# A two-layer hybrid model on one core: tiles in multiples of 64 bytes, a rewritten first phase, retention products in split form, and lower weight parts set 32 bytes further on

## The chip, the core and the metric

The program runs on one core of a Trainium2 chip. The metric is the device time of one execution in microseconds. The profile shows the engines TensorE (PE; its weight loads are listed apart as PEld), VectorE (DVE), ScalarE (ACT), GpSimd (POOL) and SyncE (SP, which here only issues transfers), and the DMA engines.

## What is computed

Two transformer layers on 256 tokens with 2048 features, batch 1, all in float32. Cut to what matters:

```python
def reference(x, mem, positions, ...):
    mem_n = _rmsnorm(mem, norm_mem)
    h = x
    for l in range(2):
        hn = _rmsnorm(h, norm_mix[l])
        if l == 0: h = h + _mixer_ab(hn, ...)  # 8 block-attention heads and 8 sparse-attention heads, then w_out_ab
        else:      h = h + _mixer_c(hn, ...)   # 8 retention heads: q, k of 256, v of 512 features, then w_out_c
        h = h + _cross_attn(_rmsnorm(h, norm_cross[l]), mem_n, ...)  # 4 heads on 256 memory rows
        h = h + _conv_ffn(_rmsnorm(h, norm_ffn[l]), ...)             # 2048 -> 2 x 5632, width-3 convolution, gate, -> 2048
    return _rmsnorm(h, norm_final)
...
    def step(state, xs):                       # retention, chunks of 128 tokens
        qi, ki, vi = xs
        intra = einsum('bhnm,bhmv->bhnv', einsum('bhnd,bhmd->bhnm', qi, ki) * decay, vi)
```

## The kernel before

Every weight is streamed from HBM once. A float32 product is made of three matmuls in the type float32r. `weights` loads a tile of 128 x 1024 values (`raw`), ScalarE rounds it to its upper part (`hi`, L232) and VectorE takes the rest as its lower part (`lo`, L233). Activations are split likewise into one slab of 128 x 512 values per 128 features: 256 columns (tokens) of the upper part, 256 of the lower. The names of tiles in a profile are all "t"; "acc" is a pair of accumulators in PSUM for the big products, "bank" a PSUM tile for the small ones.

There are two forms of a product. In `product_b` the weights are stationary: the upper part is loaded as weights and the whole slab of 512 columns streams past it (L272, upper times upper and upper times lower); then the lower part is loaded, and only the 256 columns of the slab's upper part stream past (L277). Eight slabs make a chunk: 16 matmuls of L272 and 16 of L277, in turns. In `product_a` the slab is stationary, and the weights' upper, lower and upper part stream past it (L307, L308, L309), with 512 columns, or with 256 and 280 in the first two products of the first layer. Small products (transposes, attention, retention) use plain float32, of which each matmul shows as two records in the trace (the transposes as one).

The tile allocator places tiles at multiples of 32 bytes. As built, slabs and weight parts all begin 32 bytes past a multiple of 64. In the product of 280 columns, weights lie 1120 bytes apart in a tile, so that they start in turns at 32 and at 0 past a multiple of 64.

**First phase** (L363 to L414). Two products with w_in_ab (columns 4096 to 4607, the compressed keys' and values' inputs) run in step with the loading of x. `SPANS` gives pairs of slabs; for each pair x and the weights are loaded on SP's queue, x is split (L197 on ScalarE, L200 on VectorE), the weights are split (L401, L406, L407), and `first` issues the pair's matmuls. From the ninth slab on, x is loaded ahead, and weights come four slabs at a time. The results leave the accumulators by `halves` (L326 on ScalarE, L328 on VectorE). The two products use all four accumulators, so the product behind them (columns 4864, L307) waits for `halves`. The order of ScalarE, VectorE and TensorE is that of the code here, and in the rest of the program TensorE's is, while the other engines' order is the scheduler's.

**Side work.** `side` is a queue of generators; `run` advances the first n of them by one step after each step of the big product, and so their small matmuls stand between the big ones. `start_steps` loads the rows of x for the first norm (`load_rows`), sums their squares (`norm.add`, L148), and builds tables; `compress`, `nsa_group`, `nsa_head` and `angle_steps` are such generators.

**Retention** (`mixer_c`). Per head `ev_v` brings v out of PSUM (L963) and subtracts its mean (L965). `attend` makes the scores (L975, L977), multiplies them by the decay (L979, L980), and multiplies scores and v in float32 (L986, L988).

Of the kernel before, what the change touches and what calls it, by code (L numbers as in the profile page):

```python
# [20 lines left out]
P = 128  # L21
# [54 lines left out]
def hybrid_kernel(ctx: ExitStack, tc: tile.TileContext, a, out):  # L76
# [33 lines left out]

    ident = new([P, P])
    make_identity(nc, ident)
    ones = new([P, P])
    pool.memset(ones, 1.0)
# [98 lines left out]


# [150 lines left out]
    SPANS = [range(k, k + 2) for k in range(0, ND, 2)]  # L365
# [5 lines left out]
    def load_x(p):  # L371

        nc.sync.dma_start(x_in[p].rearrange("p s t -> p (s t)"), a["x"][:, 2 * p * S : (2 * p + 2) * S])
# [5 lines left out]
    with tc.manual_schedule(engines=engines):  # L379
        act.activation(new([P, 1]), eps, AF.Copy, scale=eps)  # L380
        load_par(nc.sync, "mix")
        for p in range(ND // 2):
            i, c = p // 2, slice(p % 2 * 512, p % 2 * 512 + 512)
            if p % 2 == 0:
                raws = [raw_tile() for _ in range(2)]
                his = [new([P, 1024], F32R, "whi", 4) for _ in range(2)]
                los = [new([P, 1024], F32R, "wlo", 4) for _ in range(2)]
            if p < 4:
                load_x(p)
            for q in range(2):  # L390
                if p < 4 or p % 2 == 0:
                    d = c if p < 4 else slice(0, 1024)
                    nc.sync.dma_start(raws[q][:, d], w_ab.part(4 * i, 4, 4096 + 256 * q, 256)[:, d])
            if p == 3:
                for x in range(4, 8):
                    load_x(x)
            for s in (2 * p, 2 * p + 1):
                xs_mix.append(slab_tile())
                xhat_hi(xs_mix[s], x_in[p][:, s % 2, :], gain("mix")[:, s : s + 1])
            if p == 0:  # L400
                dve.tensor_copy(his[0][:, c], raws[0][:, c])  # L401
            for s in (2 * p, 2 * p + 1):
                xhat_lo(xs_mix[s], x_in[p][:, s % 2, :], gain("mix")[:, s : s + 1])
            for q in range(2):
                if p or q:
                    act.activation(his[q][:, c], raws[q][:, c], AF.Copy)  # L406
                dve.tensor_sub(los[q][:, c], raws[q][:, c], his[q][:, c].bitcast(F32))  # L407
# [3 lines left out]
            if p == 3:  # L411
# [126 lines left out]
    def cross(l, xs, norm, head_done):  # L538
# [24 lines left out]
        for blk in range(2):  # L563
            run(product_b_steps(weights(w_q, 0, ND, 2 * P * blk, 2 * P), xs, ev_q), n=4)
# [52 lines left out]
    def mixer_ab(xs, row, col, kcv):  # L617
# [6 lines left out]
        def start_steps():  # L624
            norm = Norm()
            tg = [(t, g) for g in range(4) for t in range(2)]
            for i in range(10):
                if i < 8:
                    load_rows(*tg[i])
                if i > 1:  # L630
                    norm.add(*tg[i - 2])
                if i < 9:
                    yield
# [8 lines left out]
            yield from angle_steps(0, posi)  # L642
# [19 lines left out]
        def compress(i, kind, t, done):  # L662

            for _ in range(8):
# [79 lines left out]
        side.extend((start_steps(), setup_steps()))  # L744
# [23 lines left out]
        def nsa_group(g, qr, qu):  # L768
# [34 lines left out]
            yield  # L803
            yield
            yield
# [4 lines left out]
            dve.tensor_copy(pct, b[:, 0:S])  # L810
            pcts[g] = pct

        def nsa_head(g, r, q):
# [9 lines left out]
            while len(comp) < 2:  # L823
# [104 lines left out]
    def mixer_c(xs, norm, done):  # L928
# [25 lines left out]
        def head(h, os):  # L954
# [4 lines left out]
            v = [long(), long()]  # L959

            def ev_v(t, acc):
                sm = small(1)
                act.activation(v[t], acc, AF.Identity, scale=norm.c[:, t : t + 1], accum_out=sm)  # L963
                dve.tensor_scalar_mul(sm, sm, -1.0 / 512)
                dve.tensor_scalar_add(v[t], v[t], sm)  # L965
# [247 lines left out]
```

## Time and profile before

| | before |
|---|---|
| median of 3 runs | 2832.78 us (2832.66 to 2833.45) |
| the profiled execution | 2834.51 us, span 2832.8 us, mean granted clock 0.998 |
| TensorE busy | 2812.4 us of the span, 14726 matmuls |
| VectorE, ScalarE busy | 1906.3 us, 1460.1 us |
| DMA | 530.11 MB, mean 187 GB/s |

Matmuls are pipelined, and their ends are modelled: the time that one costs in a stream is the distance to the start of the next, not its duration. A row of the timeline gives start, duration, engine, line, operation, tiles and shapes, the number of merged instructions and, in brackets, the idle time before and what ended it.

### The profile page before, as it was taken

How to read it: one execution, taken by the hardware profiler on the slowest of the kernel's cores; microseconds unless marked ns; L12 is line 12 of the kernel's file. 1: busy time of each engine (PE TensorE's matmuls, PEld its weight loads, DVE VectorE, ACT ScalarE, POOL GpSimd, SP SyncE). 2: the span in 40 equal slices, each digit the busy share in tenths (PEclk: the TensorE clock that was granted, in tenths of full speed). 3: DMA queues.
4: the chain of work that ended last, by engine and by line, in shares of the span. 5: the costliest groups of instructions: out<-in, count | busy, mean ns of one | idle time of the engine just before them, and what ended most of it. 6: DMA issues, size and time to landing. Idle time of an engine off the chain costs nothing.

```text
span 2832.8 us, 39488 instructions
## 1 busy us (share of the span) xinstructions
PE 2812.4 (99%) x14726; PEld 2406.5 (85%) x14726; DVE 1906.3 (67%) x3147; ACT 1460.1 (52%) x2193; POOL 29.9 (1%) x211
## 2 busy tenths in 40 slices
PE   8999999999999999999999999999999999999998
PEld 7888888888888888888888888888888888888887
DVE  7765776776767677665555555556767767676766
ACT  6454455654545455454444444444665645454544
POOL 0000000000000000000000000000000000000000
PEclk9999999999999999999999999999999999999999
DMA  8535565455555555555555555555545555555554
GB/s 305 171 126 161 180 211 172 170 189 192 187 198 190 189 196 201 194 179 179 179 178 186 193 178 179 182 206 189 189 164 193 186 196 184 193 193 187 197 186 158
DMA packets 150544, 530.11 MB, mean 187 GB/s; under 512 B 17040, under 2 KB 17456, under 8 KB 150352
## 3 DMA queue, kind: packets, MB, share of 16 engines
q1 hardware_dynamic: 148752, 523.65, 54.7%
q0 software_dynamic: 1024, 2.90, 0.3%
q8 instruction: 115, 1.88, 0.3%
q10 hardware_dynamic: 576, 1.05, 0.1%
q14 instruction: 77, 0.63, 0.1%
HBM read 525.43 MB, written 2.10 MB: 186 GB/s over the span
## 4 chain that ended last, share of the span: by engine, by line
PE 98%; DMA 1%; ACT 0%; DVE 0%; SPq 0%; issue 0%; ACTq 0%; DVEq 0%
PE acc L272 32%; PE acc L277 17%; PE acc L307 14%; PE acc L309 14%; PE acc L308 14%; PE bank L350 1%; PE bank L986 0%; DMA t<-in_w_in_ab_dram 0%; PE bank L504 0%; PE bank L496 0%; PE bank L484 0%; DMA t<-in_rows_dram 0%; PE bank L1009 0%; PE bank L589 0%; PE bank L579 0%; PE bank L975 0%
## 5 line engine op out<-in xcount | busy, mean ns | idle before, releaser
L233 DVE TENSOR_TENSOR t<-t,t 128x1024 fp32r<-128x1024 f32 x954 | 1156.6, 1220 | 568.7 <-ACT t L232 522.9
L232 ACT ACTIVATE t<-t 128x1024 fp32r<-128x1024 f32 x954 | 1004.6, 1057 | 739.6 <-PE acc L309 540.6
L272 PE MATMUL acc<-t,t 128*128 128x512 f32 x4096 | 965.9, 391 | 6.2 <-DVE t L200 6.2
L272 PEld LDWEIGHTS acc<-t,t 128*128 128x128 f32 x4096 | 759.7, 188 | 159.1 <-DVE t L200 6.2
L307 PE MATMUL acc<-t,t 128*128 128x512 f32 (+2 forms) x1824 | 713.3, 391 | 4.9 <-DVE t L328 4.9
L309 PE MATMUL acc<-t,t 128*128 128x512 f32 (+2 forms) x1824 | 705.1, 387 | 0.0
L308 PE MATMUL acc<-t,t 128*128 128x512 f32 (+2 forms) x1824 | 704.5, 386 | 0.0
L277 PEld LDWEIGHTS acc<-t,t 128*128 128x128 f32 x4096 | 510.6, 192 | 11.6 <-issue 0.4
L277 PE MATMUL acc<-t,t 128*128 128x256 f32 x4096 | 518.0, 283 | 0.0
L307 PEld LDWEIGHTS acc<-t,t 128*128 128x128 f32 x1824 | 343.9, 189 | 74.7 <-DVE t L328 5.4
L309 PEld LDWEIGHTS acc<-t,t 128*128 128x128 f32 x1824 | 343.6, 188 | 69.5
L308 PEld LDWEIGHTS acc<-t,t 128*128 128x128 f32 x1824 | 343.9, 189 | 68.9 <-issue 1.9
L883 ACT ACTIVATE t<-acc 128x256 f32<-128x256 f32 x176 | 65.8, 374 | 229.6 <-PE acc L272 229.6
L886 DVE TENSOR_TENSOR t<-acc,t 128x256 f32<-128x256 f32 x176 | 74.1, 421 | 157.2 <-ACT t L883 157.2
L889 ACT ACTIVATE t<-t,t 128x256 f32<-128x256 f32 x176 | 103.8, 590 | 1.1
L210 ACT ACTIVATE t<-t 128x256 fp32r<-128x256 f32 x88 | 36.1, 411 | 130.5 <-DVE t L908 130.5
L607 DVE TENSOR_TENSOR t<-t,acc 128x512 f32<-128x512 f32 x148 | 95.1, 680 | 2.8 <-PE acc L1104 2.8
L891 DVE SCALAR_TENSOR_TENSOR t<-t,t,t 128x256 f32<-128x256 f32 x176 | 84.2, 478 | 1.5
L890 DVE SCALAR_TENSOR_TENSOR t<-t,t,t 128x256 f32<-128x256 f32 x176 | 84.2, 478 | 0.2
L326 ACT ACTIVATE t<-acc 128x256 f32<-128x256 f32 x80 | 30.0, 376 | 103.4 <-PE acc L272 103.4
L328 DVE TENSOR_TENSOR t<-acc,t 128x256 f32<-128x256 f32 x80 | 33.4, 419 | 69.7 <-ACT t L326 69.7
L887 DVE TENSOR_TENSOR t<-t,t 128x256 f32<-128x256 f32 x176 | 74.3, 422 | 3.0
(218 smaller groups left out, 1127.6 us busy)
## 6 DMA issues: line engine op xcount, KB each, us to landing
t<-in_w_up_dram SPq DMA_DIRECT2D x352, 512.0 KB, 3.4
t<-in_w_in_c_dram SPq DMA_DIRECT2D x192, 512.0 KB, 3.5
t<-in_w_down_dram SPq DMA_DIRECT2D x176, 512.0 KB, 3.4
t<-in_w_in_ab_dram SPq DMA_DIRECT2D x80, 512.0 KB, 4.2
t<-in_w_out_c_dram SPq DMA_DIRECT2D x64, 512.0 KB, 3.3
t<-in_w_out_ab_dram SPq DMA_DIRECT2D x32, 512.0 KB, 4.2
t<-in_w_kv_x_dram SPq DMA_DIRECT2D x32, 512.0 KB, 3.8
t<-in_w_q_x_dram SPq DMA_DIRECT2D x16, 512.0 KB, 3.2
```

What stands on the lines that cost most here:

```text
L232: act.activation(hi[:, 0 : m * ncol], raw[:, 0 : m * ncol], AF.Copy)
L233: dve.tensor_sub(lo[:, 0 : m * ncol], raw[:, 0 : m * ncol], hi[:, 0 : m * ncol].bitcast(F32))
L272: pe.matmul(acc[j], parts[k - k0][0][:, j * P : (j + 1) * P], xs[k], start=(k == 0), stop=(end and k == n - 1))
L277: pe.matmul(acc[j][:, 0:S], parts[k - k0][1][:, j * P : (j + 1) * P], xs[k][:, 0:S], start=False, stop=(end and k == n - 1))
L307: pe.matmul(o, xh, hi, start=(k == 0), stop=False)
L308: pe.matmul(o, xh, lo, start=False, stop=False)
L309: pe.matmul(o, xl, hi, start=False, stop=(k == n - 1))
L607: dve.tensor_add(part(t, g), part(t, g), acc)
L887: dve.tensor_mul(u[:, 2:], t, norm.r)
L889: act.activation(c, u[:, 2:], AF.Identity, bias=cp[:, 3, j : j + 1], scale=cp[:, 2, j : j + 1])
L890: dve.scalar_tensor_tensor(c, u[:, 1 : S + 1], cp[:, 1, j : j + 1], c, op0=ALU.mult, op1=ALU.add)
L891: dve.scalar_tensor_tensor(c, u[:, 0:S], cp[:, 0, j : j + 1], c, op0=ALU.mult, op1=ALU.add)
```

## The change

Four things change.

1. `new` rounds the rows of two-dimensional tiles up to a multiple of 64 bytes. As built, slabs and weight parts now begin at a multiple of 64 bytes. `part_tile` makes the split weights' tiles, and in `product_b` and in the first phase the lower parts begin 8 values (32 bytes) into theirs; upper parts and all parts in `product_a` do not.
2. The first phase: eight matmuls of ones run ahead; the first two spans are single slabs; x and weights are loaded span by span in the order of use, the first weights on ScalarE's queue.
3. Side work: the rows' loads begin one step later and their sums four steps later; `angle_steps` becomes a generator of its own behind `setup_steps`; `compress` begins six steps earlier; `nsa_group` and `nsa_head` yield at other places.
4. Retention: v and the decayed scores are split into upper and lower parts, and each float32 matmul becomes three in float32r.

```diff
     def new(shape, dt=F32, tag=None, bufs=1):
...
+        unit = 64 // mybir.dt.size(dt)
+        if len(shape) == 2 and shape[1] % unit:
+            full = [shape[0], -(-shape[1] // unit) * unit]
+            return sb.tile(full, dt, name=name, tag=tag or name, bufs=bufs)[:, 0 : shape[1]]
...
+    def part_tile(tag, shift=0):
+        return new([P, 1040 if tag == "wlo" else 1024], F32R, tag, 4)[:, shift : shift + 1024]
...
-    def weights(w, s0, ns, c0, ncol):
+    def weights(w, s0, ns, c0, ncol, shift=0):
...
-            raw, hi, lo = raw_tile(), new([P, 1024], F32R, "whi", 4), new([P, 1024], F32R, "wlo", 4)
+            raw, hi, lo = raw_tile(), part_tile("whi"), part_tile("wlo", shift)
...
     def product_b(w, xs, c0, evac, s0=0, n=2):
-        run(product_b_steps(weights(w, s0, len(xs), c0, 2 * P), xs, evac), n=n)
+        run(product_b_steps(weights(w, s0, len(xs), c0, 2 * P, 8), xs, evac), n=n)
...
-    SPANS = [range(k, k + 2) for k in range(0, ND, 2)]
+    SPANS = [range(0, 1), range(1, 2)] + [range(k, k + 2) for k in range(2, ND, 2)]
...
+        warm = bank()
+        for _ in range(8):
+            pe.matmul(warm[:, 0:P], ones, ones, start=True, stop=True)
...
+        for ks in SPANS:
...
+            load_x(ks[0], ks[0] + m)
             for q in range(2):
...
+                (nc.sync if ks[0] else nc.scalar).dma_start(raws[q][:, d], w_ab.part(ks[0] // 4 * 4, 4, 4096 + 256 * q, 256)[:, c])
+            if ks[0] == 0:
+                load_par(nc.sync, "mix")
...
         def start_steps():
...
-            for i in range(10):
-                if i < 8:
-                    load_rows(*tg[i])
-                if i > 1:
-                    norm.add(*tg[i - 2])
-                if i < 9:
-                    yield
+            for i in range(14):
+                if 0 < i < 9:
+                    load_rows(*tg[i - 1])
+                if i > 5:
+                    norm.add(*tg[i - 6])
+                yield
...
         def compress(i, kind, t, done):
-            for _ in range(8):
+            for _ in range(2):
                 yield
...
-            v = [long(), long()]
+            vh, vl = [[new([P, 512], F32R, *tag) for _ in range(2)] for tag in (("vh", 2), ("long", 9))]
 
             def ev_v(t, acc):
-                sm = small(1)
-                act.activation(v[t], acc, AF.Identity, scale=norm.c[:, t : t + 1], accum_out=sm)
+                sm, v = small(1), new([P, 512], F32, "p", 7)
+                act.activation(v, acc, AF.Identity, scale=norm.c[:, t : t + 1], accum_out=sm)
                 dve.tensor_scalar_mul(sm, sm, -1.0 / 512)
-                dve.tensor_scalar_add(v[t], v[t], sm)
+                act.activation(vh[t], v, AF.Identity, bias=sm)
+                dve.scalar_tensor_tensor(vl[t], v, sm, vh[t].bitcast(F32), op0=ALU.add, op1=ALU.subtract)
...
+                ph, pl = new([P, 512], F32R, "p", 7), new([P, 512], F32R, "p", 7)
+                act.activation(ph[:, 0 : S + P], pr[:, 0 : S + P], AF.Copy)
+                dve.tensor_sub(pl[:, 0 : S + P], pr[:, 0 : S + P], ph[:, 0 : S + P].bitcast(F32))
...
-                    pe.matmul(b, pr[:, t * P : (t + 1) * P], v[0], start=True, stop=(t == 0))
-                    if t:
-                        pe.matmul(b, pr[:, S : S + P], v[1], start=False, stop=True)
+                    blocks = [(t * P, 0), (S, 1)][: t + 1]
+                    for c0, i in blocks:
+                        for p_, v_ in ((ph, vh), (ph, vl), (pl, vh)):
+                            pe.matmul(b, p_[:, c0 : c0 + P], v_[i], start=(i == 0 and p_ is ph and v_ is vh),
+                                      stop=(c0 == blocks[-1][0] and p_ is pl))
```

Where the change moves instructions, the order of an engine's queue shows it. First SP's queue at the very start, before the change (t_72 holds the gains, t_75 and t_76 are x, t_92 and t_93 the raw weights of the two products):

```order
L128 DMA t_72<-in_par_dram 128x32
L373 DMA t_75<-in_x_dram 128x512
L393 DMA t_92<-in_w_in_ab_dram 128x512
L393 DMA t_93<-in_w_in_ab_dram 128x512
L373 DMA t_76<-in_x_dram 128x512
```

and with it (L381 loads x, L133 the gains, L408 the weights):

```order
L381 DMA t_75<-in_x_dram 128x256
L133 DMA t_72<-in_par_dram 128x32
L381 DMA t_75<-in_x_dram 128x256
L408 DMA t_102<-in_w_in_ab_dram 128x256
L408 DMA t_103<-in_w_in_ab_dram 128x256
```

x now stands ahead of the gains, and the first slab's two weight loads have left SP's queue for ScalarE's, where they are the first two instructions.

Next ScalarE's queue at the end of the first phase, before (L148 sums the squares of a row tile, t_73 and t_74 are the rows; L232 splits weights; L326 evacuates an accumulator):

```order
L148 ACTIVATE t_464,t_408<-t_74 128x512 [waits DMAHW6_49]
L148 ACTIVATE t_485,t_408<-t_73 128x512 [waits DMAHW7_49]
L232 ACTIVATE t_391<-t_390 128x1024 [waits DMAHW0_49,DVE_49,PE_49]
L148 ACTIVATE t_500,t_408<-t_74 128x512 [waits DMAHW2_49]
L232 ACTIVATE t_431<-t_430 128x1024 [waits DMAHW1_49,DVE_49,PE_49]
L148 ACTIVATE t_521,t_408<-t_73 128x512 [waits DMAHW4_49]
L148 ACTIVATE t_538,t_408<-t_74 128x512 [waits DMAHW5_49]
L326 ACTIVATE t_346<-acc_111 128x256 [waits PE_49]
L326 ACTIVATE t_350<-acc_112 128x256 [waits PE_49]
```

and with the change (L153, L241 and L335 are these three lines now):

```order
L421 ACTIVATE t_307<-t_348 128x512 [waits DMAHW3_49]
L241 ACTIVATE t_415<-t_414 128x1024 [waits DMAHW4_49,DVE_49,PE_49]
L153 ACTIVATE t_550,t_432<-t_73 128x512 [waits DMAHW5_49]
L335 ACTIVATE t_370<-acc_117 128x256 [waits PE_49]
L241 ACTIVATE t_454<-t_453 128x1024 [waits DMAHW6_49,DVE_49]
L335 ACTIVATE t_374<-acc_118 128x256 [waits PE_49]
L153 ACTIVATE t_573,t_432<-t_74 128x512 [waits DMAHW7_49]
L153 ACTIVATE t_606,t_432<-t_73 128x512 [waits DMAHW0_49]
```

One sum of squares stands ahead of the first evacuation now, where six did (one of them earlier than the rows shown).

Last TensorE's queue at the products of scores and v in one head, before:

```order
L986 MATMUL bank2611_12704<-t2563_12479,t2603_12664 128x512 [waits DVE_49]
L986 MATMUL bank2613_12709<-t2563_12479,t2603_12664 128x512
L988 MATMUL bank2613_12709<-t2564_12480,t2603_12664 128x512 [waits DVE_49]
L307 MATMUL acc2598_12639<-t2622_12735,t2465_12053 128x512 [waits Activation_49]
```

and with it (t2613 and t2614 are the scores' upper and lower part, t2568 and t2570 those of v's first half, t2569 and t2571 of its second):

```order
L1008 MATMUL bank2622_12738<-t2568_12503,t2613_12697 128x512 [waits Activation_49]
L1008 MATMUL bank2622_12738<-t2570_12505,t2613_12697 128x512 [waits DVE_49]
L1008 MATMUL bank2622_12738<-t2568_12503,t2614_12698 128x512 [waits DVE_49]
L1008 MATMUL bank2624_12745<-t2568_12503,t2613_12697 128x512
L1008 MATMUL bank2624_12745<-t2570_12505,t2613_12697 128x512
L1008 MATMUL bank2624_12745<-t2568_12503,t2614_12698 128x512
L1008 MATMUL bank2624_12745<-t2569_12504,t2613_12697 128x512
L1008 MATMUL bank2624_12745<-t2571_12506,t2613_12697 128x512
L1008 MATMUL bank2624_12745<-t2569_12504,t2614_12698 128x512
```

Three matmuls have become nine at the same place, and the first ones now wait for ScalarE's and VectorE's splits.

More of the change, by code (lines that the diff above doesn't have):

```diff
@@ L108, in slab_tile @@
         return new([P, 2 * S], F32R, "xs", 32)
+    ones = new([P, P])
+    pool.memset(ones, 1.0)
     ident = new([P, P])
     make_identity(nc, ident)
-    ones = new([P, P])
-    pool.memset(ones, 1.0)
     eps = new([P, 1])
@@ L379, in hybrid_kernel @@
     with tc.manual_schedule(engines=engines):
[L380 to L384, printed above, removed]
+        warm = bank()
+        for _ in range(8):
+            pe.matmul(warm[:, 0:P], ones, ones, start=True, stop=True)
+        raws = [None, None]
+        for ks in SPANS:
+            p, m = ks[0] // 2, len(ks)
+            c = slice(ks[0] % 4 * 256, ks[0] % 4 * 256 + 256 * m)
+            if ks[0] % 4 == 0:
+                his = [part_tile("whi") for _ in range(2)]
+                los = [part_tile("wlo", 8) for _ in range(2)]
+            if ks[0] in (0, 4, 14):
                 raws = [raw_tile() for _ in range(2)]
[L386 to L389, printed above, removed]
+            elif ks[0] in (8, 10, 12):
+                raws = [new([P, 512], F32, "p", 7) for _ in range(2)]
+            d = slice(0, 512) if ks[0] in (8, 10, 12) else c
+            load_x(ks[0], ks[0] + m)
             for q in range(2):
[L391 to L397, printed above, removed]
+                (nc.sync if ks[0] else nc.scalar).dma_start(raws[q][:, d], w_ab.part(ks[0] // 4 * 4, 4, 4096 + 256 * q, 256)[:, c])
+            if ks[0] == 0:
+                load_par(nc.sync, "mix")
+                act.activation(new([P, 1]), eps, AF.Copy, scale=eps)
+            for s in ks:
                 xs_mix.append(slab_tile())
@@ L400, in hybrid_kernel @@
             if p == 0:
-                dve.tensor_copy(his[0][:, c], raws[0][:, c])
-            for s in (2 * p, 2 * p + 1):
+                dve.tensor_copy(his[0][:, c], raws[0][:, d])
+            for s in ks:
                 xhat_lo(xs_mix[s], x_in[p][:, s % 2, :], gain("mix")[:, s : s + 1])
@@ L563, in cross @@
         for blk in range(2):
-            run(product_b_steps(weights(w_q, 0, ND, 2 * P * blk, 2 * P), xs, ev_q), n=4)
+            run(product_b_steps(weights(w_q, 0, ND, 2 * P * blk, 2 * P, 8), xs, ev_q), n=4)
         while len(xm) < ND:
@@ L641, in start_steps @@
                     dve.tensor_mul(kcv[i][:, j, :], held[i][j], row)
-            yield from angle_steps(0, posi)
             dve.tensor_copy(cos_k, row)
@@ L802, in nsa_group @@
             side.extend(nsa_head(g, r, qr[r]) for r in range(4))
-            yield
-            yield
-            yield
+            for _ in range(6):
+                yield
             b = bank()
@@ L810, in nsa_group @@
             dve.tensor_copy(pct, b[:, 0:S])
+            yield
+            yield
             pcts[g] = pct
@@ L822, in nsa_head @@
             yield
-            while len(comp) < 2:
+            while len(comp) < 2 or g not in pcts:
                 yield
@@ L1078, in finish @@
                     if g > 1:
-                        hi, lo = new([P, 1024], F32R, "whi", 4), new([P, 1024], F32R, "wlo", 4)
+                        hi, lo = part_tile("whi"), part_tile("wlo")
                         act.activation(hi, raw, AF.Copy)
```

13 lines of the change are left out of this document (7 added, 6 removed).

## The prediction

> **What bounds the kernel now.** I read the page's busy shares and its chain first, then the groups by line, then single stretches of the timeline to get the spacing of the matmuls, because a pipelined matmul's duration says little. "L272" is the upper part of a weight (512 columns stream past it), "L277" the lower part (256 columns), L307 to L309 the three matmuls of the other product.
>
> ```profile
> PE 2812.4 (99%) x14726; PEld 2406.5 (85%) x14726; DVE 1906.3 (67%) x3147; ACT 1460.1 (52%) x2193; POOL 29.9 (1%) x211
> PE 98%; DMA 1%; ACT 0%; DVE 0%; SPq 0%; issue 0%; ACTq 0%; DVEq 0%
> L272 PE MATMUL acc<-t,t 128*128 128x512 f32 x4096 | 965.9, 391 | 6.2 <-DVE t L200 6.2
> L307 PE MATMUL acc<-t,t 128*128 128x512 f32 x1760 | 693.5, 394 | 0.0
> L277 PE MATMUL acc<-t,t 128*128 128x256 f32 x4096 | 518.0, 283 | 0.0
> ```
>
> TensorE is busy for 99% of the span and 98% of the chain is its own; all waits on other engines that the waits view lists are the two quoted further on. So only two things shorten the run: a smaller spacing of matmuls, or less idle or slow-clocked time at the start. The spacing, from starts in the timeline:
>
> ```profile
> 639.63 4.70 PE L272 MATMUL acc<-t,t 128*128 128x512 f32 x20
> 644.16 4.00 PE L277 MATMUL acc<-t,t 128*128 128x256 f32 x32
> 647.99 3.82 PE L272 MATMUL acc<-t,t 128*128 128x512 f32 x16
> 36.27 0.41 PE L309 MATMUL acc<-t,t 128*128 128x256 f32 x1
> 36.91 0.41 PE L309 MATMUL acc<-t,t 128*128 128x256 f32 x1
> 1304.17 1.88 PE L986 MATMUL bank<-t,t 128*128 128x512 f32 x4
> 1305.89 1.02 PE L988 MATMUL bank<-t,t 128*128 128x512 f32 x2
> 1306.97 0.40 PE L308 MATMUL acc<-t,t 128*128 128x512 f32 x1
> ```
>
> Upper: 4.53/20 = 226.5 ns. Lower: 3.83/32 = 119.7 ns. The 256 further columns cost 106.8 ns, 0.417 ns each, so each matmul also has 12.9 ns that do not depend on its columns. At half clock that share is gone: three 256-column matmuls take 0.64 us, 213 ns or 0.833 ns a column and nothing more. Plain float32 has hardly any either: 1.72/4 = 430 ns for 512 columns at 0.84 ns. So the 12.9 ns look less like a fixed cost than like two reads getting in each other's way, that of the columns at full speed and that of the next weights, and some 13,500 matmuls pay it.
>
> **Part 1, the first phase.** What the trace shows of the start:
>
> ```profile
> PE acc L272 <- DVE t L200: 6.2, 1, 6.2
> PE acc L307 <- DVE t L328: 4.9, 1, 4.9
> 10.29:30.58 20.29, 20.29 (x118) 17.60 (x116) 13.37 (x33) 14.36 (x31) 3.63 (x9) 1.00 1.01 359
> 30.58:35.67 5.09, 0.15 (x1) 0.00 (x0) 2.35 (x4) 3.89 (x10) 0.00 (x0) 0.85 0.97 358
> 35.67:41.00 5.33, 5.33 (x25) 5.33 (x26) 4.29 (x11) 3.42 (x8) 0.00 (x0) 0.50 0.78 267
> 400.00:1100.00 700.00, 700.00 (x3767) 608.29 (x3767) 496.22 (x781) 379.97 (x574) 8.41 (x85) 1.00 0.55 186
> 0.74 0.38 SPq L128 DMA_DIRECT2D t<-in_par_dram  x1
> 1.18 0.42 SPq L373 DMA_DIRECT2D t<-in_x_dram  x1
> 1.65 0.90 SPq L393 DMA_DIRECT2D t<-in_w_in_ab_dram  x2
> 8.07 1.06 PE L277 MATMUL acc<-t,t 128*128 128x256 f32 x4
> 10.48 1.11 PE L277 MATMUL acc<-t,t 128*128 128x256 f32 x8
> 34.17 0.63 ACT L148 ACTIVATE t<-t 128x512 f32<-128x512 f32 x1 [0.25 <-DMA t<-in_rows_dram]
> 34.80 0.64 ACT L326 ACTIVATE t<-acc 128x256 f32<-128x256 f32 x2
> ```
>
> (Stretches: length, busy time of PE, PEld, DVE, ACT, POOL, then granted clock, DMA share, GB/s.) Four terms. (a) The first matmul starts at 6.2. The first x and weights are now half as large, x goes ahead of the gains, and the two weights leave by ScalarE's queue at once instead of third and fourth behind SP's slots of 0.4 us: about 1.5 us earlier. (b) Until about 10.3 matmuls run at half clock: at 8.07 four lower ones last 1.06 us, less 0.42 for the last 0.64/3 = 213 ns apart, at 10.48 eight last 1.11, less 0.28 0.83/7 = 119. That loses some 2 us; the eight matmuls on ones now run ahead of the data, each 128 columns in two passes, 0.43 us at half clock, 3.4 us in all. I take 1.5 of the 2. (c) The wait of 5.09 us: the next product needs the accumulators, whose evacuation L326 stood on ScalarE behind L148, which waited for the rows' DMA until 34.17. In the new order L326's counterpart comes earlier, and three of the four ahead-standing row sums go behind; what is left are one weight split of 1.06 us (L232 below) and its subtraction: about 1.5 us. Gain 3.6. (d) That pause lets the clock fall: 0.50 from 35.67 to 41.00, half of 5.33 = 2.7 us lost, no more if the pause is short. Sum 9.3. Against it stands the DMA column: share 1.01 at 359 GB/s, so the transfers are at their limit and data will be late next. I take 7 of the 9.3; ends 2 (transfers give back nearly all) and 10. The moves of the compression's loads, the angle steps and the short yields lie beside busy TensorE with SP's queue as cover (DMA share 0.55 from 400 on); I cost them at nothing, plus or minus 2 if an accumulator or the compressed values come late.
>
> **Part 2, split retention values.** Per head two L986 and one L988, each recorded twice: from 1304.17 to 1306.74 (the start of L308 less one spacing), 2.57 us. Instead there are nine of 226.5 ns, 2.04 us: 0.53 us, times 8 heads = 4.2 us. The added splits lie on other engines:
>
> ```profile
> 1300.13 0.28 DVE L980 TENSOR_TENSOR t<-bank,t 128x128 f32<-128x128 f32 x1
> 1505.47 0.69 ACT L963 ACTIVATE t<-acc,t 128x512 f32<-128x512 f32 x1 [0.30 <-PE acc L309]
> 1294.55 0.49 DVE L965 TENSOR_SCALAR t<-t,t 128x512 f32<-128x512 f32 x1
> 1504.11 1.06 ACT L232 ACTIVATE t<-t 128x1024 fp32r<-128x1024 f32 x1 [1.66 <-PE acc L309]
> ```
>
> ScalarE gets two copies of 0.69 and one of 384 values (about 0.5), VectorE one subtraction of 384 (about 0.5) and two longer forms in place of two of 0.49. Scores are done at 1300.41, the products start at 1304.17: 3.8 us cover 1.0. Behind the two copies on ScalarE waits L232, which itself idled 1.66 us for a free buffer. If the cover were gone, 1.0 x 8 = 8 us back; ends -4.2 and +4. I take -4.2.
>
> **Part 3, lower weights 32 bytes on.** Before, columns and weights of every lower matmul start at 32 beyond a multiple of 64; after, columns at 0, weights at 32. No row shows such a pair at 256 columns. What rows show of the 12.9 ns:
>
> ```profile
> 17.95 0.63 PE L277 MATMUL acc<-t,t 128*128 128x256 f32 x4
> 18.42 2.02 PE L272 MATMUL acc<-t,t 128*128 128x512 f32 x8
> 49.62 0.29 PE L307 MATMUL acc<-t,t 128*128 128x280 f32 x1
> 50.38 0.29 PE L307 MATMUL acc<-t,t 128*128 128x280 f32 x1
> 51.16 0.29 PE L307 MATMUL acc<-t,t 128*128 128x280 f32 x1
> 51.93 0.29 PE L307 MATMUL acc<-t,t 128*128 128x280 f32 x1
> 175.99 3.92 PE L272 MATMUL acc<-t,t 128*128 128x512 f32 x16
> 179.75 2.08 PE L277 MATMUL acc<-t,t 128*128 128x256 f32 x16
> ```
>
> A group of four after uppers takes 0.47 us, 117.5 each; if the last three go at 119.7, the first takes 111. Same shape, same kind of address, less time: the conflict depends on how the two reads lie to each other in time. An offset of 32 bytes changes just that, and since 256 columns and 128 weights are whole multiples of 64 bytes, the pattern repeats in each matmul and a good position stays. Against it: at 280 columns the columns' start alternates between 32 and 0 beyond 64 every six matmuls, and the groups take 0.76, 0.78 and 0.77 us, no difference; but 280 columns are 17.5 times 64 bytes, so there the position drifts anyhow. Ends: all 12.9 ns gone, 4096 x 12.9 = -53 us; doubled, +53. I take 113 ns, between 111 and 117.5 and nearer to the group's first: 4096 x 6.7 = -27 us.
>
> **Part 4, tiles of 64 bytes.** For the 512-column matmuls both starts move by 32 together. Nothing in the rows moves with a common offset, so I take nothing. Ends: 4096 + 3 x 1760 = 9376 such matmuls lose all 12.9 ns, -121 us; or all go as the worst stretch shown, 3.76/16 = 235 ns, +80 us.
>
> Sum: -7 - 4.2 - 27 = -38.2. The profiled execution took 2834.5, 1.7 above its span and above the median of 2832.8: it would come to 2796.3, the median to 2794.6.
>
> **Rivals.** R1: neither offset matters, TensorE's two reads do not meet, and only parts 1 and 2 count: 2832.8 - 11.2 = 2821.6. For it speak the 280-column rows; against it the missing 12.9 ns at half clock. The Trainium skill, page "SBUF — State Buffer", section "Who interferes with whom", gives TensorE two independent read ports and says that it never waits on anyone; by that rule parts 3 and 4 are zero and the time is R1's. The trace agrees with it for plain float32 (430 ns), not for the 119.7 that were 111 once.
>
> R2: a start off a multiple of 64 itself costs, so the 512-column ones gain as well. With 6.7 ns each, 9376 x 6.7 = 63 us more than forecast: 2732; with all 12.9 ns gone from both kinds, 2648. For it: both operands of all these matmuls stand off by 32 now, so the trace holds no aligned pair to deny it. Against: the 280-column groups. The same skill, page "TensorE: Matmul & The Clock Gate", section "Back-to-back issue gap", has N/2.4 + 2.5 ns between warm matmuls taken alone, 109.2 and 215.8 here; by it the time would be an estimate of some 2675. The quoted spacings do not agree with it.
>
> R3, slower: the offset puts the weights' read where it meets more of the columns'. If the lower ones take 6.7 ns more, 126.4, that is +27 - 11.2: 2849. It decides from 119.7 + 11.2/4.096 = 122.4 ns on. For it: 235 ns at 175.99 shows that worse positions exist. Against: only stretches behind float32 work show it, and they recover.
>
> R4: transfers hold the start and give back more than part 1 gains, some 3 us lost instead of 7 won; with part 3 as forecast 2805, inside its range.
>
> **How the numbers follow.** Forecast 0.45 (own range 2775 to 2815: lower ones at 109 to 117.5, start 2 to 10); R1 0.22 (2815 to 2829); R2 0.18 (2648 to 2750); R3 0.10 (2834 to 2870); all else, R4 without part 3 among it, 0.05. A change of 0.2%, 5.7 us, is about what a measurement of this kernel tells from none. Faster by more: 0.45 + 0.18 + 0.19 of R1 + 0.02 = 0.84; within: 0.03 + 0.03 = 0.06; slower: R3's 0.10. The range goes from 2690, which leaves out the lower half of R2, to 2834, which leaves out R3.
>
> **What would show it.** Part 1: no wait above 2 us of the first product on the evacuation's VectorE step, first real matmul near 4.7, no stretch at clock 0.50 near 36. Part 2: nine matmuls in 2.04 us a head without a pause. Part 3: spacing of the lower ones at 113 (119.7: R1; above 122.4: R3). Part 4: uppers at 226.5 (220 or less: R2). I am wrong if the lower ones stay at 119.7, or if uppers move.

## The result: 1% slower, 28.7 us

| | before | after |
|---|---|---|
| median | 2833.11 us (4 runs, 2832.66 to 2834.89) | 2861.77 us (4 runs, 2861.58 to 2863.47) |
| span of the profiled execution | 2832.8 us | 2859.8 us |

The ratio is 1.0102, with an interval of 1.0087 to 1.0117. The forecast was 2795, with 2690 to 2834: the result lies outside the range, on its upper side.

The page of after, its busy time, chain and main groups (columns as before; L281 is the former L272, L286 the former L277, L316 to L318 the former L307 to L309):

```profile
PE 2846.4 (100%) x14766; PEld 2408.9 (84%) x14766; DVE 1913.4 (67%) x3158; ACT 1479.1 (52%) x2218; POOL 30.1 (1%) x211
PE 99%; DVE 0%; DMA 0%; ACT 0%; issue 0%; SPq 0%
L281 PE MATMUL acc<-t,t 128*128 128x512 f32 x4096 | 984.2, 397 | 0.7 <-ACT t L421 0.5
L316 PE MATMUL acc<-t,t 128*128 128x512 f32 (+2 forms) x1824 | 717.0, 393 | 1.1 <-DVE t L337 1.1
L286 PE MATMUL acc<-t,t 128*128 128x256 f32 x4096 | 511.8, 281 | 0.3
```

TensorE idles less than before and yet is busy for 34 us more. The time is not in a wait but in the matmuls. All waits of PE that the waits view of after lists, against 6.2 and 4.9 us before:

```profile
PE acc L316 <- DVE t L337: 1.1, 2, 0.8
PE bank L499 <- DVE t L491: 1.0, 1, 1.0
PE bank L392 <- POOL t L117: 1.0, 1, 1.0
PE acc L281 <- ACT t L421: 0.5, 1, 0.5
PE acc L281 <- DVE t L205: 0.2, 1, 0.2
```

The spacing shows in the timeline of after, from start to start:

```profile
601.67 7.63 PE L281 MATMUL acc<-t,t 128*128 128x512 f32 x32
609.13 3.94 PE L286 MATMUL acc<-t,t 128*128 128x256 f32 x32
612.91 7.63 PE L281 MATMUL acc<-t,t 128*128 128x512 f32 x32
```

Thirty-two uppers take 7.46 us, 233.1 ns each (226.5 in the forecast's rows of before), and 32 lower ones 3.78 us, 118.1 ns each (119.7 before). The lower ones, which were to gain 6.7 ns, gained some 1.5; the uppers, which were to stay, lost more than 6.

What the built kernels show explains where to look. Call *distance* the start of the streamed columns less the start of the stationary weights, in bytes within a partition. Before, every weight part and every slab began at 288 modulo 512, so the distances of the big products' 512- and 256-column matmuls were multiples of 512. After, the upper parts begin at 320 modulo 512 and the slabs at 128: the one-value tile, now of 64 bytes, stands between weights and slabs, and the four buffers of the lower parts have grown by 64 bytes each. So the uppers of `product_b` stand at 320 (64 modulo 256), those of `product_a` at 192, and the lower parts at another distance in each of their four buffers (those of the 256-column matmuls at 32, 96, 160 and 224 modulo 256).

### The profile page after: what moved, and what is told of

Its sections match the earlier page's. It is cut to its first block, busy times and chain, and to the rows that moved or that the text cites. A ratio compares the mean times of both kernels' runs of the same rounds, so it can differ in the third digit from the quotient of the medians.

```text
span 2859.8 us, 39615 instructions
## 1 busy us (share of the span) xinstructions
PE 2846.4 (100%) x14766; PEld 2408.9 (84%) x14766; DVE 1913.4 (67%) x3158; ACT 1479.1 (52%) x2218; POOL 30.1 (1%) x211
## 3 DMA queue, kind: packets, MB, share of 16 engines
q0 software_dynamic: 1024, 2.90, 0.3%
## 4 chain that ended last, share of the span: by engine, by line
PE 99%; DVE 0%; DMA 0%; ACT 0%; issue 0%; SPq 0%
PE acc L281 33%; PE acc L286 17%; PE acc L316 15%; PE acc L317 15%; PE acc L318 15%; PE bank L359 1%; PE bank L1008 1%; PE bank L519 0%; PE bank L511 0%; PE bank L499 0%; PE bank L1030 0%; PE bank L991 0%; PE bank L604 0%; PE bank L594 0%; PE bank L509 0%; DMA t<-in_w_in_ab_dram 0%
## 5 line engine op out<-in xcount | busy, mean ns | idle before, releaser
L241 ACT ACTIVATE t<-t 128x1024 fp32r<-128x1024 f32 x954 | 1008.5, 1058 | 743.7 <-PE acc L318 534.7
L281 PE MATMUL acc<-t,t 128*128 128x512 f32 x4096 | 984.2, 397 | 0.7 <-ACT t L421 0.5
L281 PEld LDWEIGHTS acc<-t,t 128*128 128x128 f32 x4096 | 761.6, 189 | 167.6 <-ACT t L421 1.0
L316 PE MATMUL acc<-t,t 128*128 128x512 f32 (+2 forms) x1824 | 717.0, 393 | 1.1 <-DVE t L337 1.1
L318 PE MATMUL acc<-t,t 128*128 128x512 f32 (+2 forms) x1824 | 710.7, 390 | 0.0
L286 PEld LDWEIGHTS acc<-t,t 128*128 128x128 f32 x4096 | 503.8, 188 | 13.6 <-DVE t L422 0.9
L286 PE MATMUL acc<-t,t 128*128 128x256 f32 x4096 | 511.8, 281 | 0.3
L318 PEld LDWEIGHTS acc<-t,t 128*128 128x128 f32 x1824 | 342.7, 188 | 77.6
L316 PEld LDWEIGHTS acc<-t,t 128*128 128x128 f32 x1824 | 342.6, 188 | 77.7 <-DVE t L337 1.5
L215 ACT ACTIVATE t<-t 128x256 fp32r<-128x256 f32 x88 | 36.1, 410 | 128.1 <-DVE t L922 128.1
L335 ACT ACTIVATE t<-acc 128x256 f32<-128x256 f32 x80 | 30.0, 377 | 102.4 <-PE acc L281 100.7
```

The lines of the kernel that those rows point to most:

```text
L241: act.activation(hi[:, 0 : m * ncol], raw[:, 0 : m * ncol], AF.Copy)
L281: pe.matmul(acc[j], parts[k - k0][0][:, j * P : (j + 1) * P], xs[k], start=(k == 0), stop=(end and k == n - 1))
L286: pe.matmul(acc[j][:, 0:S], parts[k - k0][1][:, j * P : (j + 1) * P], xs[k][:, 0:S], start=False, stop=(end and k == n - 1))
L316: pe.matmul(o, xh, hi, start=(k == 0), stop=False)
L318: pe.matmul(o, xl, hi, start=False, stop=(k == n - 1))
```

## The experiments

In all tables U is the mean spacing of the 512-column matmuls of `product_b`, A that of the 512-column ones of `product_a`, L that of the 256-column ones, in ns: the differences of successive starts in a trace, with steps over 300 ns (waits and other work between) left out. There are some 4050, 5220 and 4090 of them. These means are worked out from the traces' starts; no view lists them. Each ratio is to runs of before taken beside that kernel, whose medians are 2832.77 to 2833.57. The theory (D): the spacing depends on the distance. Its rivals: the absolute start at a multiple of 64 bytes (M), or the shift by 32 bytes alone (S).

| kernel | U | A | L | median, us | ratio to before, interval |
|---|---|---|---|---|---|
| before | 227.8 | 227.1 | 120.4 | 2833.11 | |
| after | 232.3 | 231.8 | 118.9 | 2861.77 | 1.0102, 1.0087 to 1.0117 |
| a_abs32 | 227.8 | 227.1 | 120.5 | 2832.51 | 0.9999, 0.9989 to 1.0009 |
| b_rel320 | 229.2 | 233.3 | 117.2 | 2856.92 | 1.0085, 1.0070 to 1.0100 |
| c_after_rel0 | 227.8 | 227.1 | 120.4 | 2825.40 | 0.9975, 0.9966 to 0.9984 |
| f_no_shift | 229.3 | 233.3 | 116.9 | 2850.64 | 1.0063, 1.0046 to 1.0080 |
| g_tiny_first | 228.2 | 230.5 | 118.9 | 2838.86 | 1.0021, 1.0012 to 1.0031 |
| p3_lo32 | 228.5 | 227.1 | 119.0 | 2829.93 | 0.9988, 0.9980 to 0.9997 |
| p3_lo192 | 228.2 | 227.1 | 118.5 | 2826.93 | 0.9978, 0.9969 to 0.9987 |
| d_ret | 227.8 | 227.1 | 120.4 | 2829.51 | 0.9986, 0.9977 to 0.9995 |
| e_best64 | 227.7 | 227.1 | 118.2 | 2816.65 | 0.9943, 0.9931 to 0.9956 |
| e_pad64 | 227.8 | 231.9 | 118.2 | 2842.32 | 1.0035, 1.0021 to 1.0049 |

### All of before, 32 bytes further on (a_abs32)

```diff
+    new([P, 8])
     ident = new([P, P])
```

> The kernel before with one unused tile of 32 bytes ahead of all others, so that every slab and weight part starts at a multiple of 64 bytes as in the changed kernel, while the distances between the tiles stay as before (columns and weights differ by a multiple of 512 bytes everywhere). Theory D (the distance between the two starts within 512 bytes sets the spacing; 0 in the kernel before, 192 to 384 in the changed one): 2833 us, uppers at 227 ns. Theory M (a start at a multiple of 64 is itself the worse one): uppers at 231 to 233 ns, 2833 + 9376 x 5 ns = about 2880 us. Theory S (only the 32-byte shift of the lower parts slows the stream): 2833.

The starts are now at 0 modulo 64, as after, and the distances are those of before. 2832.51 against 2833.11 us, and the same three spacings within 0.1 ns: M falls.

### Before, with 320 unused bytes between weights and slabs (b_rel320)

```diff
                 los = [new([P, 1024], F32R, "wlo", 4) for _ in range(2)]
+                if p == 0:
+                    new([P, 80])
```

> The kernel before with 320 unused bytes between the weights' tiles and the slabs: absolute starts stay at 32 past a multiple of 64, but the columns of an upper matmul of product_b now start 320 bytes past its weights within 512, those of product_a 192, as in the changed kernel. Theory D: uppers at 231 to 234 ns as in the changed kernel, lower ones at 117 to 120, so 2833 + 9376 x 5 ns - 4096 x 2 ns = about 2870 us. Theories M and S: 2833 us, uppers at 227.

23.8 us slower, with no instruction changed and no part shifted. In its timeline (L272 uppers, L277 lower ones) the uppers take 7.33/32 = 229.1 ns and the lower ones 3.62/32 = 113.1 in the first stretch, 118 in the next:

```profile
603.55 7.49 PE L272 MATMUL acc<-t,t 128*128 128x512 f32 x32
610.88 3.79 PE L277 MATMUL acc<-t,t 128*128 128x256 f32 x32
614.50 7.48 PE L272 MATMUL acc<-t,t 128*128 128x512 f32 x32
621.83 3.93 PE L277 MATMUL acc<-t,t 128*128 128x256 f32 x32
625.60 4.74 PE L272 MATMUL acc<-t,t 128*128 128x512 f32 x20
```

Displacing slabs against weights is enough; S falls as an account of the loss. The direction is theory D's, its 2870 us is missed by 13: A and L came as expected (233.3 and 117.2), but U rose to 229.2 only, not to 231 or more. The uppers of after, at the same distance, take 232.3; there the lower parts between them stand elsewhere.

### The changed kernel with the distances of before (c_after_rel0)

```diff
-        return new([P, 1040 if tag == "wlo" else 1024], F32R, tag, 4)[:, shift : shift + 1024]
+        return new([P, 1024], F32R, tag, 4)
...
-        raws = [None, None]
+        raws, tiny = [None, None], new([P, 1])
...
-                act.activation(new([P, 1]), eps, AF.Copy, scale=eps)
+                act.activation(tiny, eps, AF.Copy, scale=eps)
```

> The changed kernel (its first phase, side order, split retention and tiles of 64 bytes kept), but lower parts without shift in tiles of 1024 values, and the one-value tile of the first phase placed ahead of the weights, so that columns and weights differ by a multiple of 512 bytes again. Theory D: uppers at 227, lower ones at 120, and only the first phase (-7) and the retention (-4) are left: about 2822 us. Theory M: uppers stay at 232, 2862 to 2870 us. Theory S: 2822 as well, but then the run with 320 bytes is at 2833.

2825.40 us, 7.7 below before and 3.4 above theory D's 2822, since the first phase brought less than 7 (see below). The timeline has 7.28/32 = 227.5 and 3.83/32 = 119.7 ns again:

```profile
609.46 7.44 PE L281 MATMUL acc<-t,t 128*128 128x512 f32 x32
616.74 4.00 PE L286 MATMUL acc<-t,t 128*128 128x256 f32 x32
620.57 7.44 PE L281 MATMUL acc<-t,t 128*128 128x512 f32 x32
```

Against this kernel the changed one has nothing but its placement, and the account closes: summed over the traces, U takes 939.7 instead of 922.0 us, A 1211.1 instead of 1186.5, L 486.4 instead of 492.6: +17.7 + 24.6 - 6.2 = +36.1. The medians differ by 36.4.

### Which displacement costs what (f_no_shift, g_tiny_first)

The first undoes part 3 alone (buffers of 1024 values, no shift), the second only moves the one-value tile back ahead of the weights:

```diff
 f_no_shift:
-        return new([P, 1040 if tag == "wlo" else 1024], F32R, tag, 4)[:, shift : shift + 1024]
+        return new([P, 1024], F32R, tag, 4)
 g_tiny_first:
-        raws = [None, None]
+        raws, tiny = [None, None], new([P, 1])
...
-                act.activation(new([P, 1]), eps, AF.Copy, scale=eps)
+                act.activation(tiny, eps, AF.Copy, scale=eps)
```

> The changed kernel without its part 3: buffers of the lower parts of 4096 bytes again and no shift; the one-value tile stays behind the weights, so all distances are 64 modulo 256 for product_b and 192 for product_a. Theory D: spacings as where 320 bytes stood between weights and slabs, 229.2, 233.3 and 117.2 ns, so that run's 2856.9 less the 7.7 of first phase and retention: 2849 (2845 to 2853), and part 3 is then to be charged with 10 to 17 us of the changed kernel's time. If part 3 brought a gain also in this layout, as the forecast has it, this run is above the changed kernel, 2862 or more.

> The changed kernel with the one-value tile ahead of the weights again; part 3 as changed (4160-byte buffers, 32 bytes of shift). Upper parts at a multiple of 256 bytes; the lower parts of product_a at 0, 64, 128 and 192 by buffer, the 256-column ones at 32, 96, 160 and 224. Theory D with mixing (in the run with 64 bytes of pad, product_a's mean rose from 227.1 to 231.9 though two thirds of it stood at a multiple of 256): uppers of product_b 227.8, product_a 230 to 232 (up 15 to 25 us), lower ones 118.9 (down 6), from the 2825.4 at distance 0: 2834 to 2845. Without mixing, only the shifted third of product_a counts: three buffers of four at 229 to 233 instead of 227, 5 to 8 us, less 6: 2825 to 2828.

From the 2825.40 at distance 0, the moved tile alone costs 25.2 us (2850.64) and the widened, shifted buffers alone 13.5 (2838.86); together they cost 36.4, so they nearly add. The three spacings of f_no_shift are those of b_rel320 within 0.3 ns, although one stands at 64 and 448 modulo 512 and the other at 320 and 192: the pattern repeats after 256 bytes. In g_tiny_first the uppers are at a multiple of 256 and only the lower parts stand elsewhere; A still rises by 3.4 ns over all of it, and the matmuls of L316 and L318, whose own distance is a multiple of 256, take 230.8 and 229.3 ns. A matmul whose own distance is good loses here when its neighbours' is not.

### The lower parts alone (p3_lo32, p3_lo192)

Before, with part 3 as the only change: the buffers of the lower parts are widened by whole 512 bytes, so that nothing else is displaced.

```diff
+    def lo_tile(shift=0):
+        return new([P, 1152], F32R, "wlo", 4)[:, shift : shift + 1024]
...
-        run(product_b_steps(weights(w, s0, len(xs), c0, 2 * P), xs, evac), n=n)
+        run(product_b_steps(weights(w, s0, len(xs), c0, 2 * P, 8), xs, evac), n=n)    # p3_lo192: 48
```

> The kernel before with the lower parts of the weights for 256-column matmuls 32 bytes further on, their buffers widened by a whole 512 bytes so that every other distance between a matmul's columns and its weights stays a multiple of 512 bytes. Forecast's part 3: lower matmuls from 119.7 to 113 ns, 4096 of them, 27 us less (2806). Theory D (what counts is the distance of the two starts modulo 256 bytes, and the map's row for the lower ones at this distance, 224, has 118.2 against 118.7 ns at 0; the wider buffers alone change nothing): the 512-column matmuls stay at 227 ns, the lower ones go from about 120 to 117.5 to 118.5 ns, 4 to 10 us less (2823 to 2829). A third theory, that a shift of the lower parts also slows the upper ones that stand next to them: the 512-column matmuls over 229 ns and the time above 2835.

> The same with the lower parts 192 bytes further on instead of 32, which puts the columns 64 bytes behind a multiple of 256 from the weights, the distance at which the lower matmuls had 116.3 ns where 320 bytes stood between the weights and the slabs. Theory D: 4096 lower ones at 116 to 117 ns instead of 120, 12 to 16 us less (2817 to 2821), and less than with the 32 bytes. If instead any shift does the same for the lower ones, this run comes out as the run with 32 bytes, within 3 us.

The 32 bytes bring 3.5 us, 192 bytes (distance 64) 6.5. The lower ones fall by 1.4 and 1.9 ns, and the uppers next to them rise by 0.7 and 0.4. The first lands 1 us above what theory D gave and the second 6, since neither the uppers' loss nor the weaker gain of the 192 bytes beside undisturbed uppers was counted; that 192 bytes bring more than 32 is borne out.

### Retention alone (d_ret)

Before, with the changed kernel's split of `vh`, `vl`, `ph` and `pl` and its nine products, word for word as in the change.

> The kernel before with the split of the retention's value and score parts alone (three float32r matmuls for each float32 one). Forecast: 0.53 us less in each head, 4.2 us less in all (2829). Rival: since the changed first phase and the split together gave 7.7 us less and the third product alone began 7.0 us earlier, the split brings 0.7 us or nothing (2832 to 2834), because its distances (288 and 416 bytes modulo 512) are slow ones or because the longer chain of evictions makes another wait.

3.9 us less. The nine products of the first head, and what follows:

```profile
1303.76 2.25 PE L993 MATMUL bank<-t,t 128*128 128x512 f32 x9
1305.84 0.39 PE L307 MATMUL acc<-t,t 128*128 128x512 f32 x1
```

2.08 us a head instead of 2.57, and 8 x 0.49 = 3.9. The forecast's 4.2 holds, and the first phase with the moved side work is then worth 7.7 - 3.9 = 3.8 us.

### Three maps (m_map32, m_lo16, m_hi4)

In each the parts of successive weights tiles begin at other places in wider buffers, in turn; one run each, read by distance.

```diff
+    def part_pair():
+        s = [0, 1, 2, 3, 4, 5, 6, 7, 8, 9, 10, 11, 12, 13, 14, 15][turn[0] % 16] * 8    # m_lo16: % 16 * 4, lower parts alone; m_hi4: uneven steps, upper parts alone
+        turn[0] += 1
+        return [new([P, 1152], F32R, tag, 4)[:, s : s + 1024] for tag in ("whi", "wlo")]
```

> The kernel before, with the split weights in tiles of 1152 values and upper and lower part of each tile set 0, 32, 64, ... 480 bytes in, in turn, so that one trace holds all 16 distances in steps of 32 bytes. Theory D: the spacing of uppers (512 columns) and lower ones (256) depends on the distance: about 227 and 120 at 0, 230 to 237 at 192 to 384 and 117 to 120 there, and some distance may beat 227. Theories M and S: one spacing for all multiples of 64, another for the odd multiples of 32, no dependence beyond that.

> A map: the kernel before with the upper parts of the weights left where they are and the lower parts at starts of 0, 16, 32 and so on to 240 bytes in a buffer of 4608 bytes, in turn; the mean spacing of the 256-column matmuls is read for each of the 16 distances. Theory D with a step of 32 bytes: a pair of distances that lie within one 32-byte step has one spacing, and the spread of the 16 is 116 to 120 ns as in the map in which both parts moved. If the step is finer, the 16 odd distances have values of their own, and one of them may lie below 116. The 512-column uppers stay at 227 to 228 ns throughout. Time about 2825 to 2840 over all, since the lower parts of the other products, which have 512 columns, stand at slow distances in 15 of 16 buffers: some 1800 of these at up to 233 instead of 227 ns add up to 10 us.

> A map of the upper parts alone, the lower ones left where they are: starts of 0, 4, 8, 12, 16, 24, 40, 48, 80, 112, 144, 176, 208, 240, 248 and 252 bytes in a wider buffer. Theory D with a fine step: no distance beats 227 ns of the multiple of 256 for the 512-column uppers, distances of a few bytes lie between 227 and 233. If the step is 32 or 64 bytes, distances of 4 to 28 bytes on one side are as fast as 0. Time some 15 to 20 us above the kernel before, since the 9376 matmuls of 512 columns stand at slow distances in most buffers.

From m_map32 (2869.85 us), mean spacing by distance modulo 256, in stretches at one distance. Here, and in the values of the other two maps, steps over 135 ns at 256 columns are left out too; in the large table these some 35 steps add 0.7 ns to L (before: 119.7 without them):

| distance | 0 | 32 | 64 | 96 | 128 | 160 | 192 | 224 |
|---|---|---|---|---|---|---|---|---|
| U | 228.0 | 233.3 | 228.8 | 232.9 | 231.9 | 233.0 | 232.9 | 231.7 |
| L | 118.7 | 117.9 | 117.7 | 120.2 | 119.2 | 117.7 | 117.8 | 118.2 |

For 512 columns 0 and 64 stand out, and the rest costs 3.7 to 5.3 ns. Which of the two is better the map doesn't say: its stretches at 0 are of four matmuls, and their mean is 228.0 to 229.5 by which of the four are counted. The kernels that hold one distance for all their big products decide it: 227.8 at 0 (before), 229.2 at 64 (b_rel320). For 256 columns the multiple of 256 is among the worst. In m_lo16 (2852.33 us, expected 2825 to 2840; the uppers kept 228.1) neighbours 16 bytes apart differ by up to 2.6 ns (115.1 at 192, 117.7 at 208), which speaks for a step finer than 32 bytes; with the steps over 135 ns counted, the two are 116.7 and 117.7. The third, m_hi4 (2874.68 us, 41 above before for an expected 15 to 20), settles nothing: its stretches at start 0 have over 230 ns, where every kernel that stays at that distance has 227 to 229, and those at start 252 have 226.7. In stretches as short as these a matmul's spacing also depends on the distances around it.

### The best of both (e_best64, e_pad64)

The changed kernel's first phase and retention, distance 0 for 512 columns, and only the lower parts for 256 columns 64 bytes on, in buffers of 4352 bytes (one working buffer of 12 given up); and the same distance by unused bytes ahead of and behind the lower parts' buffers.

```diff
 e_best64, against c_after_rel0:
-        return new([P, 1024], F32R, tag, 4)
+        return new([P, 1088 if tag == "wlo" else 1024], F32R, tag, 4)[:, shift : shift + 1024]    # shift 16
 e_pad64, against c_after_rel0:
+                if not ks[0]:
+                    new([P, 16])
                 los = [part_tile("wlo", 8) for _ in range(2)]
+                if not ks[0]:
+                    new([P, 48])
```

> The changed kernel's first phase and retention with the distances put right: buffers of the lower parts of 4352 bytes, the 512-column matmuls at a multiple of 256 bytes, and only the lower parts for 256-column matmuls 64 bytes further on, which is distance 192, where the map of 16-byte steps had 115.1 ns; one of the 12 buffers of the 1 KB working tiles is given up for the space. Theory D: 4096 lower ones at 115 instead of 120 ns, 20 us less, and the uppers of product_b at 227.9 instead of 227.3 as in both kernels with a shift, 2.5 us more; from the 2825.4 of the kernel with distance 0 that makes 2808 (2804 to 2813), below the kernel before by 25 us. If the map's short stretches don't carry over to a product that stays at one distance, the lower ones stay at 117 to 118 and it is 2817 to 2822. If the lost buffer counts, new waits of PE for work of DVE or ACT stand in the groups.

> The same distance 192 for the lower ones by another way: 64 unused bytes ahead of the four buffers of the lower parts and 192 behind them, no wider buffers and no shift. The lower parts of the other products (512 columns, about 1800 matmuls) then stand at distance 64, where the map had 229.0 to 229.1 against 227 ns: 3.6 us more than with the shift in the buffer, so 2812 (2807 to 2817). If distances act only on the 256-column ones, the two come out alike.

e_best64 takes 2816.65 us, 16.9 below before and 45 below the changed kernel; 32 lower ones take 3.76 us, 117.5 ns each (117.5 over the whole trace too, counted as in the map), not the map's 115.1:

```profile
608.35 7.44 PE L281 MATMUL acc<-t,t 128*128 128x512 f32 x32
615.63 3.93 PE L286 MATMUL acc<-t,t 128*128 128x256 f32 x32
619.39 7.44 PE L281 MATMUL acc<-t,t 128*128 128x512 f32 x32
```

So the map's short stretch did not carry over, as the expectation's second case has it. e_pad64 missed widely: 2842.32 for an expected 2812. Its lower ones are just as good, but a third of `product_a` stands at 64 and the rest at a multiple of 256, and all of it goes at 231.9 ns, 25 us more; the two thirds at a multiple of 256 take 231.3 and 232.4 ns. That is more than the map's 229 and b_rel320's 229.2 at 64, both of them in `product_b`; no run holds all of `product_a` at 64.

## Why the prediction was wrong, step by step

**Part 4 failed, and with it the sign.** "For the 512-column matmuls both starts move by 32 together" is not what was built: slabs and upper parts moved apart, by 64 bytes modulo 256 in `product_b` and 192 in `product_a`. The second half, that a common offset moves nothing, was right (a_abs32: 0.6 us, inside the interval). Priced at nothing, the term is U +17.7 and A +24.6 = 42 us, half of its own upper end of 80. That end rested on the 235 ns stretch, and no rival took it up, although the text names moving uppers as what would make it wrong. By edits: the moved one-value tile alone (f_no_shift) adds about 6 us to U and 32 to A and takes 14 off L; with part 3's wider buffers these become +17.7, +24.6 and -6.2. The starts stand in the built kernel and could have been compared one matmul with the next; I compared each with a multiple of 64.

**Part 3 was mis-sized.** Its reading of the 12.9 ns, that they are partly two reads in each other's way, is neither shown nor denied: the spacing moves with the distance, but the pattern has a period of 256 bytes, while the 64 of the prediction came from no row. In p3_lo32 the 32 bytes bring 1.4 ns, not 6.7, and 0.7 is lost on the uppers beside them: 3.5 us, not 27. In the changed kernel the wider buffers that carry the shift displaced `product_a`'s lower parts and put the 256-column ones at four distances; g_tiny_first prices this part at 13.5 us *more* than none. The matmul of 111 ns on which the 113 rested doesn't exist in the group quoted for it. It followed only if the other three took 119.7, and the starts of the four (each row from a narrow stretch of the timeline; x2 merges the second and third) show another thing:

```profile
17.95 0.28 PE L277 MATMUL acc<-t,t 128*128 128x256 f32 x1
18.06 0.40 PE L277 MATMUL acc<-t,t 128*128 128x256 f32 x2
18.30 0.28 PE L277 MATMUL acc<-t,t 128*128 128x256 f32 x1
18.42 0.40 PE L272 MATMUL acc<-t,t 128*128 128x512 f32 x1
```

In ns they are 117, 120, 117 and 117 apart. Shorter spacings do come up, in passing (113 or 114 for some 120 of the 4096 in before, a stretch of 113.1 in b_rel320), but no kernel held such a value as its mean.

**Part 2 held**: 3.9 us for a forecast of 4.2, and no wait of the products shows in the waits view.

**Part 1 brought 3.8 us for a forecast of 7, inside its range of 2 to 10.** The rows of after:

```profile
0.99 3.78 PE L392 MATMUL bank<-t 128*128 128x128 f32 x16 [0.99 <-POOL t L117]
4.93 1.22 PE L281 MATMUL acc<-t,t 128*128 128x512 f32 x2 [0.15 <-DVE t L205]
30.14 0.39 PE L316 MATMUL acc<-t,t 128*128 128x256 f32 x1 [0.24 <-DVE t L337]
31.61 0.39 PE L316 MATMUL acc<-t,t 128*128 128x256 f32 x1 [0.84 <-DVE t L337]
42.65 0.29 PE L316 MATMUL acc<-t,t 128*128 128x280 f32 x1
10.34:30.10 19.76, 19.43 (x111) 16.64 (x109) 14.88 (x37) 15.38 (x31) 3.58 (x9) 1.00 1.05 387
30.10:42.60 12.50, 11.61 (x96) 11.41 (x97) 12.19 (x30) 9.04 (x22) 0.00 (x0) 1.00 0.95 342
```

The first real matmul comes at 4.93 (forecast 4.7), the wait of 5.09 is 0.24 + 0.84, and the clock stays at 1.00 where it had fallen to 0.50. The 280-column product starts at 42.65 instead of 49.62: 7.0 us, the forecast's number. The transfers stay at their limit (share 1.05).

That the 7.0 is met is luck. The profiled execution of before had a slow start, and the terms (c) and (d) were read from it. The profile of a_abs32, which has the instructions and the spacings of before (L308 and L329 are its L307 and L328), shows another start of the same code:

```profile
PE acc L308 <- DVE t L329: 2.3, 1, 2.3
34.00:41.00 7.00, 6.98 (x58) 6.99 (x59) 6.54 (x20) 5.14 (x10) 0.00 (x0) 1.00 0.98 325
45.62 0.29 PE L308 MATMUL acc<-t,t 128*128 128x280 f32 x1
```

The wait is 2.3 instead of 4.9 us, the clock doesn't fall, and the 280-column product starts 4.0 us earlier than the 49.62 of before. From there to the end the two executions stay 4.0 us apart (spans 2828.7 and 2832.8). What the first phase brings thus depends on which execution of before it is set against, and the profiled one, at 2834.51, stands 1.4 above the median of 2833.11. Since the executions differ only in the start, the 7.0 would be 5.6 against one at the median (an estimate).

The moved side work, which I costed at nothing plus or minus 2, takes some back as well. In c_after_rel0, with the distances of before, the 280-column product starts at 43.17, 6.45 us earlier than in before, and a `product_a` further on starts at 1021.97 instead of 1027.17, 5.2 us earlier:

```profile
49.62 0.29 PE L307 MATMUL acc<-t,t 128*128 128x280 f32 x1
1027.17 0.39 PE L307 MATMUL acc<-t,t 128*128 128x512 f32 x1
```

```profile
43.17 0.29 PE L316 MATMUL acc<-t,t 128*128 128x280 f32 x1
PE bank L499 <- DVE t L491: 1.0, 1, 1.0
1021.97 0.39 PE L316 MATMUL acc<-t,t 128*128 128x512 f32 x1
```

So 1.25 us are lost in between, inside the 2 that were allowed, and 1.0 of it is TensorE's only new wait there, that of L499 in the sparse attention for VectorE's L491. Less the 1.4 by which the profiled execution of before stands above its median, 5.2 leaves the 3.8 that the medians give.

**The rivals.** R1 was near for the first two parts (2821.6; measured without any displacement 2825.40), but its premise, that placement doesn't matter, is gone: 512 columns take 227.1 or 233.3 ns by nothing but where the operands lie (a_abs32, b_rel320). The Trainium skill, page "SBUF — State Buffer", section "Who interferes with whom", gives TensorE two independent read ports and says that it never waits on anyone. The time that follows from it for parts 3 and 4, none, is not what was measured, and the measurement decides; whether the two reads wait for each other no run shows. R2's 64-byte rule is denied by a_abs32. R3 is the side on which it ended, by another mechanism: its lower matmuls became quicker, 118.9 ns, not slower.

## What to carry to other kernels

When a change alters tile sizes or their order, compare the built addresses of the two operands of each heavy matmul, before and after, as a difference modulo 256 bytes; a tile of a few bytes between two pools of buffers can cost 1% here. The 512-column float32r stream was fastest at a difference of zero in these runs, so try that first, and pad buffers in whole 256 bytes when a shift is wanted for one user of them. And when a shift's price is read from a short stretch, measure it in a kernel that holds it throughout: three of the estimates here that came from short stretches were too good (the 113 ns of part 3, the 115.1 behind e_best64, the 229 behind e_pad64).

## What the runs showed of the hardware

The spacing of float32r matmuls depends on the distance between the columns' and the weights' starts in a partition. 512 columns take 227.1 ns at 0 and 233.3 at 192 (`product_a`), 227.8 at 0 and 229.2 at 64 (`product_b`); 256 columns take 120.4 at 0, 116.9 at 64 where the uppers stand at 64 too (f_no_shift), and 118.5 at 64 beside uppers at 0 (p3_lo192). The period is 256 bytes: distances of 64 and 320, and of 192 and 448, give the same spacings within 0.3 ns (f_no_shift, b_rel320). A common offset of 32 bytes of both changes nothing (a_abs32). The few matmuls of 280 columns, 96 in a trace, show no such dependence: 130.0, 129.5 and 128.4 ns at 0, 96 and 192 (before).

The spacing also depends on the neighbours: uppers at distance 64 took 229.3 ns when the lower ones between them stood at 64 as well (f_no_shift), and 232.3 when these stood at 32, 96, 160 and 224 (after). What in the reads makes the pattern, whether it is the weights in use or those loaded for the next matmul whose place counts, and how fine its step is below 32 bytes, stays open.
